# Up-projection groups in seven products: first sums of two groups in another tile, operand halves interleaved, one more group in the wide form

## The chip, the cores and the metric

The kernel runs on one core of one Trainium2 chip. Its engines run side by side, each in the order of its own instruction list: TensorE (PE, with its weight loads shown as PEld), VectorE (DVE), ScalarE (ACT), GpSimd (POOL) and SyncE (SP); the latter two mostly issue DMAs here. The metric is the device time of one execution in microseconds, the median over the runs.

## The reference

One layer of a streaming encoder on 512 tokens of width 1024, in float32: a mixing part (gated linear attention and forgetting attention side by side) and a feed-forward part. The change lies in the feed-forward part alone:

```python
a, val = jnp.split(rmsnorm(x, norm_ffn_g) @ w_up, 2, axis=-1)   # 1024 -> 2 x 2816
a = causal_dwconv(a, conv_w, conv_b)                            # width 3, along the tokens
return x + (jax.nn.gelu(a) * val) @ w_down                      # 2816 -> 1024
```

A final RMSNorm follows.

## The kernel before

**Precision.** Every float32 operand is split into a high and a low part (`hi` is a rounded copy, made on ScalarE; `lo` the difference, made on VectorE), and a product is three matmuls: high x high, high x low and low x high (`mm3`, lines 325 to 328). `split_next` (lines 270 to 303) does this for each piece of 1024 weight columns: a DMA brings the piece into a raw tile, line 291 casts it, line 292 subtracts. Three pairs of `wh` and `wl` tiles are in use at a time.

**The up-projection.** The 22 blocks of 128 features are worked as follows: two (`NCL`) in the plain way, `plain_products`; the other twenty in ten groups (`NSS`) of two blocks by a scheme with seven products in place of eight. x is cut in two halves of tokens (256 each, `H`) and two halves of features (four blocks of 128, `KH`), which gives x11, x12, x21, x22, and the weights are cut likewise. A step (g, p) is product p of group g: 24 matmuls of 256 columns in the narrow form (`up_product`, line 1443). Operands 1, 5, 3 lie in the tile `xo`, operands 2, 6, 7 in the tile `xw`, which held the halves `x2h` and `x2l` of x for the plain products, and operand 4 in `xc`; `split_x` (line 1337) fills them. The sums and differences y1 to y4 that some of them are made from lie in spare places of `act[0]`.

The program lists the steps by `SLOT`: (0,1), (0,5), (0,2), (0,3), (0,6), (1,1), (1,5), (0,7), (1,2), (0,4), (1,3), (1,6), (2,1) and so on. Small jobs are hung ahead of the first steps (`ahead_of`, line 1437): splits of operands, and the convolution, gelu and products of the two plain blocks. The order in which each engine gets its instructions is set when the program is built, by a planner that takes what it believes to be ready, earlier program lines first; it may put a later step ahead of an earlier one that waits.

**Accumulators.** Products 1 and 2 of a group add up in one accumulator ("x"), 5 and 3 in a second ("z"), 6, 7 and 4 in a third ("y"). "x" and "z" come from two pairs of PSUM banks (`pwide`), "y" from four single banks (`pmm`), which the plain blocks use at first. When a first product is done, `joint` (line 1468) copies the sums out, and the bank goes on to the second product. The first sums of x (p = 1) are needed in "y":

- In groups 0 and 1 they are copied into a part of `act[1]` (line 1534) and added to "y" when product 6 is done (line 1544).
- From group 2 on they are put into the bank of "y" ahead (line 1537).

`act[1]` is the tile that takes the activations of the second half of the blocks; it is first needed for them in group 4. It has the slot of the pool `x2pool` that the tile `xs` has before it, and `xs` holds x11 to x22; its last reader is the split of operand 4, hung ahead of (1,2). `s3` and `s4`, two more tiles of sums, have slots of their own; `s4` is first written for the blocks of `act[1]`.

**The wide form.** In groups 2 to 8 (`WIDE`) products 1, 2, 5 and 3 go through `wide_product` (line 1456). High and low half of the operand are streamed together as 512 columns against the high weights, and the high half once more as 256 columns against the low weights: 16 matmuls where the narrow form has 24. The result lies in two halves of a bank; `joint` copies one half out on ScalarE (line 1474) and adds the other on VectorE (line 1477). The two halves of an operand lie 1024 elements apart in `xo` and 3072 apart in `xw`.

**Afterwards.** The down-projection is done in seven products too. Its odd products take their operand from `ops[1]`, whose high part is the first 2816 elements of each partition of the first half of `xw` and whose low part those of its second half; `split_act` fills it (lines 1385 and 1386).

Of the kernel before, what the change touches and what calls it, by code (L numbers as in the profile page):

```python
# [9 lines left out]
F32R = mybir.dt.float32r  # L10
# [7 lines left out]
P = 128  # L18
T = 512
NT = T // P  # L20
D = 1024
KD = D // P
# [12 lines left out]
H = T // 2  # L35
KB = NF // 2
# [23 lines left out]
NCL = 2  # L60
NSS = (NF - NCL) // 2

WIDE = range(2, NSS - 1)
SLOT = {1: -1, 5: 0, 2: 2, 3: 4, 6: 5, 7: 8, 4: 10}

EARLY = (6, 7)
# [12 lines left out]
def c_of_piece(i):  # L79

    order = []
    for c in range(-GAHEAD, KD):
        order += ([None] if c + GAHEAD < KD else []) + ([c] if c >= 0 else [])
    return order[i] if i >= 0 else None
# [7 lines left out]
def hybrid_kernel(ctx: ExitStack, tc, xT, xt, wp, wu, wd, wf, wn, pp, aw2, fing, out):  # L92
    nc = tc.nc
    mm = nc.tensor.matmul
# [19 lines left out]
    def pmm():  # L114
        return bank("mm")

    def pax():
        return bank("ax")

    def pwide():  # L120
        return banks_of["wide"].tile([P, 2, 512], F32, tag="wide", name="ps_wide")
# [47 lines left out]
    for i, w in enumerate(wps[16:n_out]):  # L169
        fresh(w)  # L170
        c = c_of_piece(i - GH - KD)
# [147 lines left out]
    def piece(ahead=NW):  # L319
        n = taken[0]  # L320
        taken[0] += 1
        split_to(n + ahead + sum(i in spare for i in range(n, n + ahead)))
        return splits[n]
# [51 lines left out]
    for _ in range(NWARM):  # L375
        mm(  # L376
            warm, lhsT=nc.const_aps.tensor(1.0, (P, P), BF16), rhs=nc.const_aps.tensor(1.0, (P, T), BF16),
            start=True, stop=True,
# [59 lines left out]

    xpool = ctx.enter_context(tc.tile_pool(name="xpool", bufs=1))

    xw = xpool.tile([P, 2, (KD - 2) * T], F32R, name="xw")
    xab = [xw[:, i] for i in range(2)]
    xc = [xpool.tile([P, 1024], F32R, name=f"xc{i}") for i in range(2)]
    xh, xl = (
        [xab[i][:, k * T : (k + 1) * T] for k in range(KD - 2)] + [c[:, i * T : (i + 1) * T] for c in xc]
# [33 lines left out]
    first = [pmm(), pmm(), pmm(), pmm(), pax()]  # L479
# [335 lines left out]
    for tt in range(NT):  # L815
        for j in range(2):
            t = slice(tt * P, (tt + 1) * P)
            c = slice((2 * (tt % 2) + j) * P, (2 * (tt % 2) + j + 1) * P)
# [15 lines left out]
    for tt in range(NT):  # L834
        for j in range(2):
            for par in range(2):
                for c in range(2 * tt, min(2 * tt + 2, NC - 1)):
# [3 lines left out]
                        lhsT=kdt[r, tt, j, par * CH : (par + 1) * CH],  # L841
                        rhs=vg[r, tt, (2 * j + par) * GDV : (2 * j + par + 1) * GDV],
                        start=True, stop=True,
# [35 lines left out]
    for u in range(2):  # L879
        for par in range(2):  # L880
            for t2, j, c in quarters:
# [4 lines left out]
                    rhs=vg[:, 2 * u + t2, h * GDV : (h + 1) * GDV],  # L886
                    start=(t2 == j == 0), stop=False, skip_group_check=True,
                )
    for u in range(2):
        for t2, j, c in quarters:  # L890
            for par in range(2):
                r = slice(par * CH, (par + 1) * CH)
                for cp in range(2):
# [3 lines left out]
                        rhs=prev[r, j, ck, :], start=False, stop=True, skip_group_check=True,  # L897
# [171 lines left out]
    for i, run in enumerate(RUNS):  # L1069
        for unit in units[2 * i : 2 * i + 2]:  # L1070
            last = logits(*unit)
        for what in run:
# [4 lines left out]
            n = int(what[1:])  # L1077
# [43 lines left out]
    def minus_sum(out, a, b):  # L1121
        nc.vector.scalar_tensor_tensor(out=out, in0=a, scalar=-1.0, in1=b, op0=ALU.mult, op1=ALU.subtract)
# [17 lines left out]
    for c in range(-GAHEAD, KD):  # L1140
# [23 lines left out]
        else:  # L1164
            k = c - KD // 2
# [146 lines left out]
    for g in range(2):  # L1312
        n = at_step[g, 5]
# [13 lines left out]

    KH = KD // 2
    xo = npool.tile([P, 6 * KH * H], F32R, tag="xo", name="xo")
    places2 = [xo[:, i * 2048 : (i + 1) * 2048].rearrange("p (a n) -> p a n", a=2) for i in range(3)]  # L1330
    places2 += [xw[:, :, i * 1024 : (i + 1) * 1024] for i in range(3)]
    both = {p: x.rearrange("p a (k t) -> p a k t", t=H) for p, x in zip((1, 5, 3, 2, 6, 7), places2)}
    xops = {p: (x[:, 0], x[:, 1]) for p, x in both.items()}
    xops[4] = tuple(x.rearrange("p (k t) -> p k t", t=H) for x in xc)
    x11, x12, x21, x22 = (xs[:, j * KH : (j + 1) * KH, i * H : (i + 1) * H] for i in range(2) for j in range(2))

# [8 lines left out]
    def block(name, n=1, pool=npool):  # L1345
        return pool.tile([P, n, KB, H], F32, tag=name, name=name)

    act = [block("act1", 2)]
# [3 lines left out]
    s3, s4 = (block(f"s{i}")[:, 0] for i in (3, 4))  # L1352
# [35 lines left out]
    def convolve(f, i, t0):  # L1388
        nonlocal last_gelu
        nc.scalar.activation(  # L1390
            out=t0[:, i], in_=ap[:, i, 2 : T + 2], func=AF.Identity, scale=col(C_CW + 2 * NF + f), bias=col(C_CB + f)
        )
        for w in (1, 0):
            nc.vector.scalar_tensor_tensor(
                out=t0[:, i], in0=ap[:, i, w : w + T], scalar=col(C_CW + w * NF + f), in1=t0[:, i],
                op0=ALU.mult, op1=ALU.add,
            )
        with tc.issue_after(last_sigmoid.ins):
            last_gelu = nc.scalar.activation(out=t0[:, i], in_=t0[:, i], func=AF.Gelu_apprx_tanh)

    def halves(x):
        return x.rearrange("p (i t) -> p i t", t=H)

    def sums_of_acts(j, k):
        if j == 0:
            nc.vector.tensor_sub(out=s3[:, k], in0=a11[:, k], in1=a21[:, k])
            split_act(0, a11, k)
        else:
            nc.vector.tensor_sub(out=s1[:, k], in0=a22[:, k], in1=a21[:, k])
            minus_sum(s2[:, k], s1[:, k], a11[:, k])  # L1410
            minus_sum(s4[:, k], a12[:, k], s2[:, k])
# [44 lines left out]
    def wide_product(ps, p, first):  # L1456

        wh, wl = piece()
        for i in range(2):
            for k in range(KH):  # L1460
                c = slice((i * KH + k) * P, (i * KH + k + 1) * P)
                mm(ps[:, i], lhsT=wh[:, c], rhs=both[p][:, :, k], start=first and k == 0, stop=False, skip_group_check=True)  # L1462
                mm(  # L1463
                    ps[:, i, 0], lhsT=wl[:, c], rhs=both[p][:, 0, k], start=False, stop=k == KH - 1,
                    skip_group_check=True,
                )

    def joint(g, ps, out=None, tag="joint3"):

        if out is None or g in WIDE:  # L1470
            x = npool.tile([P, 2, H], F32, tag=tag, name=tag, bufs=2)
            out = out or [(x, slice(0, 2))]
        if g in WIDE:
            nc.scalar.copy(out=x, in_=ps[:, :, 1])
        for o, c in out:
            if g in WIDE:
                nc.vector.tensor_add(out=o, in0=ps[:, c, 0], in1=x[:, c])
            else:
                nc.scalar.copy(out=o, in_=halves(ps)[:, c])
        return out[0][0]  # L1480
# [29 lines left out]
    def parts_of(f):  # L1510
        if f // KB == (f + 1) // KB:
            return [(f // KB, slice(f % KB, f % KB + 2), slice(0, 2))]
        return [((f + i) // KB, slice((f + i) % KB, (f + i) % KB + 1), slice(i, i + 1)) for i in range(2)]

    st_of = {}
    for n, (g, p) in enumerate(steps):
        for what in ahead_of.get(n, ()):
            what()
        st = st_of.setdefault(g, {})
        f = NCL + 2 * g  # L1520
        name = {1: "x", 2: "x", 5: "z", 3: "z", 6: "y", 7: "y", 4: "y"}[p]
        first = name not in st
        if first:

            if name == "y":
                st[name] = pmm()
            elif g in WIDE:
                st[name] = pwide().rearrange("p i (a t) -> p i a t", t=H)
            else:
                st[name] = pwide()[:, 0]  # L1530
        ps = st[name]
        (wide_product if name != "y" and g in WIDE else up_product)(ps, p, first)
        if p == 1 and g < WIDE[0]:
            st[1] = joint(g, ps, [(act[1][:, 1, KB - 2 * g - 2 : KB - 2 * g], slice(0, 2))])
        elif p == 1:
            st["y"] = pmm()
            joint(g, ps, [(halves(st["y"]), slice(0, 2))])
        elif p == 2:
            joint(g, ps, [(act[j][:, 0, k], fs) for j, k, fs in parts_of(f)])
        elif p in (3, 5):  # L1540
            st[p] = joint(g, ps, tag=f"joint{p}")
        elif p == 6:
            if g < WIDE[0]:
                nc.vector.tensor_add(out=halves(ps), in0=halves(ps), in1=st[1])
            minus_sum(ap[:, :, 2 : H + 2], halves(ps), st[3])
        elif p == 7:
            minus_sum(ap[:, :, H + 2 : T + 2], halves(ps), st[5])
            t0 = st["t0"] = npool.tile([P, 2, T], F32, tag="t0", name="t0")
            for i in range(2):
                convolve(f + i, i, t0)  # L1550
        elif p == 4:
            t0 = st["t0"]
            for i in range(2):
                for j, k, fs in parts_of(f):
                    a = act[j][:, i, k]
                    nc.vector.tensor_mul(
                        out=a, in0=a if i == 0 else halves(ps)[:, fs], in1=t0[:, fs, i * H : (i + 1) * H]
                    )
            for j, k, _ in parts_of(f):
                sums_of_acts(j, k)  # L1560
        if g == NSS - 1 and p in EARLY:
            first_down(EARLY.index(p))
# [253 lines left out]
```

## Time and profile before

| | |
|---|---|
| median of 3 runs | 698.30 us (697.53 to 698.86) |
| the profiled execution, its own time | 697.54 us |
| its span, first to last instruction | 695.8 us |
| mean granted TensorE clock | 0.994 |
| VectorE busy from 375 to 399 us | 23.49 of 24.00 us |

In the answers of the trace times are microseconds from the span's start. A row of the timeline has the start and the length of an instruction, the engine, the line of the kernel, the operation, what it writes and reads, and in brackets the time that the engine sat idle before it and what ended that. Matmuls overlap, so the distance of their starts says what one costs. A row of the waits has the waiting instruction, what released it, the time in total, how often, and the longest.

### The profile page before, as it was taken

The numbers are of one execution on the slowest core, as the hardware profiler recorded it, in microseconds if no ns is written. First come the engines' busy times: TensorE is split into PE (matmuls) and PEld (weight loads), VectorE is DVE, ScalarE is ACT, GpSimd is POOL, SyncE is SP. The second block draws the span as 40 slices with busy tenths as digits, with TensorE's granted clock in tenths as the row PEclk, the third lists the DMA queues.
The fourth block names the chain that finished last, engine by engine and source line by source line (L and its number), as shares of the span: only waits on it lengthen the run. The fifth ranks groups of instructions, "written<-read, shape, count | busy, mean of one in ns | idle before, by whom it ended". The sixth has DMA issues, their size and how long they took to land.

```text
span 695.8 us, 10697 instructions
## 1 busy us (share of the span) xinstructions
PE 683.5 (98%) x3907; PEld 588.4 (85%) x3907; DVE 546.3 (79%) x852; ACT 432.1 (62%) x698; POOL 137.0 (20%) x196
## 2 busy tenths in 40 slices
PE   9999999999999999999999799999999999999996
PEld 6788888888888888888888799999999999888885
DVE  6774979867775766677679968888998879977884
ACT  7487676677768634335675566655666666555663
POOL 1125010123321324341010111211212102000122
PEclk9999999999999999999999899999999999999999
DMA  8769398988675499978973869999899988866643
GB/s 310 270 205 310 69 286 233 301 194 213 154 166 130 112 248 216 263 138 219 242 243 90 185 129 220 214 220 206 183 231 205 211 204 243 278 200 182 194 139 121
DMA packets 46184, 142.23 MB, mean 204 GB/s; under 512 B 5396, under 2 KB 9388, under 8 KB 46004
## 3 DMA queue, kind: packets, MB, share of 16 engines
q1 hardware_dynamic: 31156, 92.98, 39.6%
q0 software_dynamic: 11808, 43.52, 35.6%
q10 hardware_dynamic: 3168, 5.05, 2.1%
q8 instruction: 30, 0.49, 0.3%
q14 instruction: 22, 0.18, 0.1%
HBM read 137.32 MB, written 27.28 MB: 237 GB/s over the span
## 4 chain that ended last, share of the span: by engine, by line
PE 97%; ACT 1%; DVE 1%; issue 0%; DVEq 0%; ACTq 0%
PE ps_mm L326 20%; PE ps_mm L328 20%; PE ps_mm L327 20%; PE ps_wide L1462 8%; PE ps_wide L326 5%; PE ps_wide L327 5%; PE ps_wide L328 5%; PE ps_wide L1463 4%; PE ps_lg L1040 1%; PE ps_lg L981 1%; PE ps_pt L1015 1%; PE ps_mm L488 1%; PE ps_ax L326 1%; PE ps_ax L327 1%; PE ps_ax L328 1%; PE ps_ax L376 1%
## 5 line engine op out<-in xcount | busy, mean ns | idle before, releaser
L291 ACT CAST wh<-rawx 128x1024 fp32r<-128x1024 f32 x75 | 76.2, 1016 | 55.9 <-PE ps_mm L327 20.0
L326 PE MATMUL ps_mm<-xw,wh 128*128 128x512 f32 (+1 forms) x320 | 109.3, 341 | 0.0
L327 PE MATMUL ps_mm<-xw,wh 128*128 128x512 f32 (+1 forms) x320 | 107.8, 337 | 0.0
L328 PE MATMUL ps_mm<-xw,wl 128*128 128x512 f32 (+1 forms) x320 | 107.6, 337 | 0.0
L292 DVE TENSOR_TENSOR wl<-rawx,wh 128x1024 fp32r<-128x1024 f32 x75 | 88.2, 1177 | 16.4 <-ACT wh L291 16.2
L292 DVE TENSOR_TENSOR wl<-raw,wh 128x1024 fp32r<-128x1024 f32 x58 | 74.6, 1287 | 20.7 <-ACT wh L291 20.5
L291 ACT CAST wh<-raw 128x1024 fp32r<-128x1024 f32 x58 | 60.7, 1048 | 41.5 <-PE ps_mm L327 19.0
L326 PEld LDWEIGHTS ps_mm<-xw,wh 128*128 128x128 f32 x320 | 60.5, 189 | 8.2 <-issue 0.9
L328 PEld LDWEIGHTS ps_mm<-xw,wl 128*128 128x128 f32 x320 | 60.5, 189 | 6.4
L327 PEld LDWEIGHTS ps_mm<-xw,wh 128*128 128x128 f32 x320 | 60.6, 189 | 5.9 <-DVE xw L1250 0.2
L1462 PE MATMUL ps_wide<-xo,wh 128*128 128x512 f32 x168 | 60.0, 399 | 0.0
L292 DVE TENSOR_TENSOR wl<-rawz,wh 128x1024 fp32r<-128x1024 f32 x31 | 39.2, 1265 | 17.0 <-ACT wh L291 16.8
L299 POOL DMA_DIRECT2D rawx<-in_wu_dram x30 | 25.9, 865 | 120.6 <-DVE wl L292 84.8
L1463 PE MATMUL ps_wide<-xo,wl 128*128 128x256 f32 x168 | 47.2, 281 | 0.0
L326 PE MATMUL ps_mm<-xc,wh 128*128 128x256 f32 (+1 forms) x136 | 45.1, 331 | 0.0
L327 PE MATMUL ps_mm<-xc,wh 128*128 128x256 f32 (+1 forms) x136 | 44.6, 328 | 0.0
L328 PE MATMUL ps_mm<-xc,wl 128*128 128x256 f32 (+1 forms) x136 | 44.5, 327 | 0.0
L291 ACT CAST wh<-rawz 128x1024 fp32r<-128x1024 f32 x31 | 32.4, 1045 | 13.6 <-issue 5.0
L307 POOL COPY tick<-wl 128x1 f32<-128x1 f32 x37 | 10.9, 295 | 136.1 <-DVE wl L292 136.1
L1462 PEld LDWEIGHTS ps_wide<-xo,wh 128*128 128x128 f32 x168 | 31.6, 188 | 7.2
L326 PE MATMUL ps_mm<-wh,xw 128*128 128x512 f32 x96 | 37.7, 393 | 0.0
L327 PE MATMUL ps_mm<-wl,xw 128*128 128x512 f32 x96 | 37.4, 390 | 0.0
(490 smaller groups left out, 1859.1 us busy)
## 6 DMA issues: line engine op xcount, KB each, us to landing
rawx<-in_wu_dram POOLq DMA_DIRECT2D x40, 512.0 KB, 6.7
rawz<-in_wp_dram SPq DMA_DIRECT2D x30, 512.0 KB, 5.3
raw<-in_wp_dram SPq DMA_DIRECT2D x22, 512.0 KB, 5.0
wsum<-in_wd_dram SPq DMA_DIRECT2D x20, 512.0 KB, 6.7
rawx<-in_wu_dram SPq DMA_DIRECT2D x20, 512.0 KB, 5.1
raw<-in_wu_dram SPq DMA_DIRECT2D x20, 512.0 KB, 4.5
rawx<-wsum SPq DMA_DIRECT2D x12, 512.0 KB, 4.5
wsum<-in_wd_dram POOLq DMA_DIRECT2D x10, 512.0 KB, 8.0
```

Of the source, the lines that this page charges most:

```text
L291: nc.scalar.copy(out=hi[:, :m], in_=raw[:, :m])
L292: nc.vector.tensor_sub(out=lo[:, :m], in0=raw[:, :m], in1=hi[:, :m].bitcast(F32))
L299: nc.gpsimd.dma_start(raw, recipes[i][0], accum_op=ALU.add)
L307: now = nc.gpsimd.tensor_copy(out=tick, in_=lo[:, 0:1].bitcast(F32))
L326: mm(ps, lhsT=ah, rhs=bh, start=start, stop=False, **k)
L327: mm(ps, lhsT=ah, rhs=bl, start=False, stop=False, **k)
L328: mm(ps, lhsT=al, rhs=bh, start=False, stop=stop, **k)
L376: mm(warm, lhsT=nc.const_aps.tensor(1.0, (P, P), BF16), rhs=nc.const_aps.tensor(1.0, (P, T), BF16), start=True, stop=True,)
L488: mm(first[i], lhsT=w[:, i * P : (i + 1) * P], rhs=x, start=(k == j == 0), stop=False)
L981: last = mm(lg[:, place_of_q(qb)], lhsT=a[r, q], rhs=b[r, :n], start=(j == 0), stop=(j == 2))
L1462: mm(ps[:, i], lhsT=wh[:, c], rhs=both[p][:, :, k], start=first and k == 0, stop=False, skip_group_check=True)
L1463: mm(ps[:, i, 0], lhsT=wl[:, c], rhs=both[p][:, 0, k], start=False, stop=k == KH - 1, skip_group_check=True,)
```

## The change

Three edits.

1. The first sums of groups 0 and 1 go into `s4` (elements 0 to 1 of its second axis for group 0, 2 to 3 for group 1) in place of `act[1]`. The bound of this way of handling them is now `PRELOADED = 2`, apart from `WIDE`.
2. `xw` becomes one flat tile, and each operand that the wide form can take lies as block, half, token: for each block of 128 features 256 elements of the high half and then 256 of the low half. `split_x` writes, and the narrow form reads, every other run of 256; the wide form's 512 columns are one run. Operand 2 now takes the first third of `xw`, 6 the second, 7 the last; before, each took a third of both halves.
3. `WIDE` begins with group 1. Group 1's products 1, 2, 5 and 3 are wide, and their joints have a copy and an add.

```diff
-WIDE = range(2, NSS - 1)
+WIDE = range(1, NSS - 1)
+PRELOADED = 2
...
-    xw = xpool.tile([P, 2, (KD - 2) * T], F32R, name="xw")
-    xab = [xw[:, i] for i in range(2)]
+    xw = xpool.tile([P, 2 * (KD - 2) * T], F32R, name="xw")
+    xab = [xw[:, i * (KD - 2) * T : (i + 1) * (KD - 2) * T] for i in range(2)]
...
-    places2 = [xo[:, i * 2048 : (i + 1) * 2048].rearrange("p (a n) -> p a n", a=2) for i in range(3)]
-    places2 += [xw[:, :, i * 1024 : (i + 1) * 1024] for i in range(3)]
-    both = {p: x.rearrange("p a (k t) -> p a k t", t=H) for p, x in zip((1, 5, 3, 2, 6, 7), places2)}
-    xops = {p: (x[:, 0], x[:, 1]) for p, x in both.items()}
+    places2 = [t[:, i * 2048 : (i + 1) * 2048] for t in (xo, xw) for i in range(3)]
+    both = {p: x.rearrange("p (k a t) -> p k a t", a=2, t=H) for p, x in zip((1, 5, 3, 2, 6, 7), places2)}
+    xops = {p: (x[:, :, 0], x[:, :, 1]) for p, x in both.items()}
...
-                mm(ps[:, i], lhsT=wh[:, c], rhs=both[p][:, :, k], start=first and k == 0, stop=False, skip_group_check=True)
+                mm(ps[:, i], lhsT=wh[:, c], rhs=both[p][:, k], start=first and k == 0, stop=False, skip_group_check=True)
                 mm(
-                    ps[:, i, 0], lhsT=wl[:, c], rhs=both[p][:, 0, k], start=False, stop=k == KH - 1,
+                    ps[:, i, 0], lhsT=wl[:, c], rhs=both[p][:, k, 0], start=False, stop=k == KH - 1,
...
-        if p == 1 and g < WIDE[0]:
-            st[1] = joint(g, ps, [(act[1][:, 1, KB - 2 * g - 2 : KB - 2 * g], slice(0, 2))])
+        if p == 1 and g < PRELOADED:
+            st[1] = joint(g, ps, [(s4[:, 2 * g : 2 * g + 2], slice(0, 2))])
...
-            if g < WIDE[0]:
+            if g < PRELOADED:
                 nc.vector.tensor_add(out=halves(ps), in0=halves(ps), in1=st[1])
```

## The prediction, made before the changed kernel ran

> **What bounds the kernel now.** I read the page first: the span, the busy shares, the chain that ended last.
>
> ```profile
> span 695.8 us, 10697 instructions
> PE 683.5 (98%) x3907; PEld 588.4 (85%) x3907; DVE 546.3 (79%) x852; ACT 432.1 (62%) x698; POOL 137.0 (20%) x196
> PE 97%; ACT 1%; DVE 1%; issue 0%; DVEq 0%; ACTq 0%
> ```
>
> TensorE is busy 98% and the chain runs through it for 97%, so an edit is worth what it takes out of TensorE's stream, or out of the few holes in it. The second view is therefore TensorE's list of waits. Its two longest entries are these, and both lie in the stretch that the change touches:
>
> ```profile
> PE ps_wide L326 <- ACT act L1479: 4.2, 1, 4.2
> PE ps_wide L326 <- ACT joint L1479: 1.4, 1, 1.4
> ```
>
> The third view is the timeline of TensorE from the first up-projection step to the first one of group 2. Columns: start, length, engine, line, what.
>
> ```profile
> 376.23 0.28 PE L326 MATMUL ps_wide<-xo,wh 128*128 128x256 f32 x1
> 376.34 0.28 PE L327 MATMUL ps_wide<-xo,wh 128*128 128x256 f32 x1
> 376.46 0.28 PE L328 MATMUL ps_wide<-xo,wl 128*128 128x256 f32 x1
> ...
> 383.54 0.39 PE L326 MATMUL ps_wide<-xo,wh 128*128 128x256 f32 x1 [1.40 <-ACT joint L1479]
> ...
> 396.60 0.58 PE L326 MATMUL ps_wide<-xw,wh 128*128 128x256 f32 x1 [4.17 <-ACT act L1479]
> ...
> 400.61 0.41 PE L326 MATMUL ps_wide<-xw,wh 128*128 128x256 f32 x1
> 400.82 0.41 PE L327 MATMUL ps_wide<-xw,wh 128*128 128x256 f32 x1
> 401.04 0.33 PE L328 MATMUL ps_wide<-xw,wl 128*128 128x256 f32 x1
> ...
> 419.04 0.40 PE L1462 MATMUL ps_wide<-xo,wh 128*128 128x512 f32 x1
> ```
>
> Three things are to be seen. Matmuls of 256 columns start 0.12 us apart, so a narrow product of 24 takes 2.88 us. The order is not that of the list of steps: after (0,1), (0,5) come (0,3), (0,6), (1,1), and (0,2), the first to read `xw`, comes only at 396.60. And after the hole of 4.17 us the matmuls start 0.21 us apart, up to 401.04: 20 intervals in 4.44 us where 2.40 would do, a loss of 2.04 us. After the hole of 1.40 us nothing is slowed.
>
> From 376.23 to 419.04 TensorE does the twelve products of groups 0 and 1: 42.81 us, of which 12 x 2.88 = 34.56 is work. **The stretch loses 8.25 us**: 1.40 + 4.17 idle, 2.04 at the slow clock, and 0.64 of drain and restart at the holes. Why the long hole is there, the timelines of ScalarE and VectorE say:
>
> ```profile
> 394.72 1.21 DVE L1341 TENSOR_TENSOR xc<-xs,xc 128x1024 fp32r<-128x1024 f32 x1
> 395.97 1.07 ACT L1479 COPY act<-ps_wide 128x512 f32<-128x512 f32 x2 [2.52 <-DVE xc L1341]
> ```
>
> The first of the two copies at 395.97 is the joint of (0,1), whose product was over by 379.1. It writes into `act[1]`, which shares its slot with `xs`, and so it waits for the last reader of `xs`, the split of operand 4 on VectorE. (0,2) accumulates in the bank that this copy reads, so it waits too; (0,7) waits behind line 1544, which needs the same sums, and (1,5) for the bank of (0,2). That wait, not VectorE's or TensorE's rate, ends last here.
>
> **The change part by part.** *First sums to `s4`.* `s4` has a slot of its own, and nothing in the kernel writes or reads it before group 4. The joint of (0,1) can then run on ScalarE as soon as the product ends, at 379.1 plus one 1.05 us cast in front of it; (0,2) needs the split of operand 2, and follows (0,5) at 382.0. What is late next? VectorE, busy nearly all the time from here:
>
> ```profile
> 376.23:382.00 5.77, 5.77 (x49) 5.70 (x47) 5.77 (x6) 5.77 (x8) 0.87 (x1) 1.00 0.55 123
> 382.00:392.30 10.30, 8.90 (x74) 8.70 (x72) 9.85 (x12) 8.51 (x11) 1.79 (x3) 1.00 0.97 213
> 392.30:401.56 9.26, 5.09 (x26) 4.96 (x25) 6.72 (x9) 2.63 (x4) 0.79 (x1) 0.63 0.53 126
> 401.56:419.04 17.48, 17.48 (x147) 17.33 (x145) 12.64 (x15) 11.33 (x15) 2.77 (x4) 1.00 0.72 146
> 419.04:439.11 20.07, 20.07 (x139) 18.58 (x138) 17.24 (x22) 12.54 (x17) 3.64 (x5) 1.00 0.91 209
> ```
>
> The columns are the stretch, its length, and the busy time of PE, PEld, DVE, ACT and POOL, then granted clock, DMA share and GB/s. VectorE does 34.98 us of work in the first four rows. The change adds four adds (line 1477) for the four wide products of group 1. The next rows give its prices:
>
> ```profile
> 380.08 1.21 DVE L1341 TENSOR_TENSOR xw<-xs,xw 128x1024 fp32r<-128x1024 f32 x1
> 381.21 1.21 DVE L292 TENSOR_TENSOR wl<-rawx,wh 128x1024 fp32r<-128x1024 f32 x1
> ...
> 391.85 0.69 DVE L1427 TENSOR_TENSOR ps_mm<-ps_mm,rb 128x512 f32<-128x512 f32 x1
> ...
> 396.58 0.70 DVE L1544 TENSOR_TENSOR ps_mm<-ps_mm,act 128x512 f32<-128x512 f32 x1
> 397.19 0.68 DVE L1406 TENSOR_TENSOR s<-act 128x512 f32<-128x512 f32 x1
> ...
> 410.28 2.73 DVE L1394 SCALAR_TENSOR_TENSOR t<-ap,ppt,t 128x512 f32<-128x512 f32 x4
> ...
> L1477 DVE TENSOR_TENSOR joint<-ps_wide,joint x14: 680/682/684, 427.0 to 558.7; 128x512 f32<-128x512 f32 x14
> ```
>
> By starts, a 1024-wide instruction holds VectorE for 1.13 us, a 512-wide one for 0.6, the four of a convolution for 2.65. I walk its queue on from 391.85, up to where I leave it as it was: line 1544 of group 0 and 1122 (1.25), operand 7 and the weights of (0,7) (2.26): 395.4, and TensorE, unbroken since 376.23, comes to (0,7) at 396.4. Then add (1,1), weights (1,2), add (1,5), 1427, weights (0,4), 1122, operand 4 (4 x 0.6 + 3 x 1.13 = 5.79): 401.2, needed at 402.1. Convolution and weights of (1,3) (3.78): 404.9, needed at 405.0. Add (1,2), 1430, weights (1,6) (2.33): 407.3, needed at 407.9. Two of 1556, 1406, 1386, weights of (2,1) (3.53): 410.8, needed at 410.7. So TensorE is met everywhere to within 0.1 us: the stall shrinks from 8.25 to a few tenths. As bounds: VectorE has 34.98 + 4 x 0.6 = 37.4 us to do in 34.5 us; if nothing can be put off TensorE waits 2.9 us, if the 2.4 us of 1556, 1406, 1386 and the 1.13 of (2,5)'s weights are put off, 33.9 is left and it waits for nothing. I take **0.5 us**, near the walk. In the last row VectorE needs 17.24 of the 20.07 us of a group, so a backlog of 2.9 is gone after one group.
>
> ScalarE (28.24 us) fits with room. The DMAs of these twelve steps keep their triggers and their order on SP and POOL (a split frees a raw tile, SP loads and POOL adds into it), and come earlier with the splits.
>
> ```profile
> rawx<-in_wu_dram POOLq DMA_DIRECT2D x40, 512.0 KB, 6.7
> ```
>
> The nearest case is (1,6): its weights are added into the tile of (1,5), split at 391.85, land 6.7 us after the issue, near 399, and are cast for 407.8. The DMA share over the four rows is 0.72 on average, 0.89 if the stretch is 34.5 us long, below the 0.91 of the last row, in which TensorE was never idle. I price them at nothing.
>
> *Group 1 wide.* From the last row a group with four wide and three narrow products takes 20.07 us, so a wide one takes (20.07 - 3 x 2.88) / 4 = 2.857 us, 0.023 less than a narrow one. The columns streamed are the same (512 + 256 against 3 x 256). Four of them: **-0.09 us**. The price is the adds, counted above, which stand in front of the release of their bank.
>
> *Halves interleaved.* The wide matmul's moving operand becomes one run of 512 instead of two of 256. What would that buy?
>
> ```profile
> L1462 PE MATMUL ps_wide<-xo,wh x168: 395/398/403, 419.0 to 555.3; 128*128 128x512 f32 x168
> ...
> 584.23 0.28 PE L328 MATMUL ps_mm<-xw,wl 128*128 128x256 f32 x1
> 584.35 0.40 PE L326 MATMUL ps_wide<-wh,acth 128*128 128x512 f32 x1
> ...
> 585.97 0.39 PE L327 MATMUL ps_wide<-wl,acth 128*128 128x512 f32 x1
> ...
> 222.14 0.39 PE L1040 MATMUL ps_lg<-ph,v 128*128 128x512 f32 x1
> 222.37 0.39 PE L1040 MATMUL ps_lg<-pl,v 128*128 128x512 f32 x1
> ```
>
> The two-run matmul of line 1462 takes 0.398, some 0.009 more than the 0.39 of other 512-wide ones. But the one-run matmul at 584.35, behind a 256-wide one as each of line 1462 is, takes 0.40 too, and line 1040's at 222.14, whose operand also has two runs, takes 0.39. So the excess goes with what stands before, not with the runs. I take 0; the bound is 256 x 0.009 = -2.3 us. The splits write in runs of 256 now; line 1341 above reads `xs` in such runs at full rate, so 0; TensorE's cover for a change there is VectorE's margin in the walk.
>
> *Operands under the last splits.* The low half of the down operand now lies where operands 6 and 7 are, not 2, 6 and 7. Two early splits on VectorE must move:
>
> ```profile
> 368.60 1.22 DVE L1370 TENSOR_TENSOR act<-xs 128x1024 f32<-128x1024 f32 x1
> ...
> 572.16 0.95 DVE L1386 TENSOR_TENSOR xw<-act,xw 128x768 fp32r<-128x768 f32 x1
> ...
> 581.36 0.95 DVE L1386 TENSOR_TENSOR xw<-act,xw 128x768 fp32r<-128x768 f32 x1
> ...
> 578.73 0.40 PE L326 MATMUL ps_wide<-wh,acth 128*128 128x512 f32 x1
> ...
> 599.52 0.39 PE L326 MATMUL ps_mm<-wh,xw 128*128 128x512 f32 x1
> ```
>
> They wait for (9,6) and (9,7) to end, at 578.73 and 584.35, where first down products start; first wanted at 599.52. Cost 0, hidden by those 15 us; bound 0.9, one of them in front of weights that TensorE then misses.
>
> **Sum**: -8.25 + 0.5 - 0.09 = -7.84 us. The profiled execution took 697.54 us, so 689.7; the median of the runs, 698.3, stands 0.76 above it, so **690.5 us**.
>
> **The rivals.** *A, the forecast*, 690.5, from 690.0 (no stall left) to 691.5; chance 0.58. *B, VectorE becomes the bound*: its queue orders what can be put off ahead of weights. For it speaks that the walk's margins are 0.1 us at (1,3) and below zero at (2,1); against it that the backlog lasts one group. 2.9 us of stall instead of 0.5: 692.9; up to 694.9 if it comes in one hole that also slows the clock by 2 us as above. Chance 0.22. The Trainium skill (page "TensorE: Matmul & The Clock Gate", section "Part 1: The HAM clock gate") says that the clock is halved after an idle window of about 3.4 us and comes back after as much work. The holes here agree with it (1.40 no, 4.17 yes, then 0.21 us for 4.4 us); by that rule B's hole of 2.9 would stay at the full clock and 692.9 would hold. *C, the single run is faster*: 0.009 us each, 2.3 us more: 688.2. For it the 0.398, against it line 1040 and 584.35. Chance 0.12. The Trainium skill (page "PSUM — Partial Sum Buffer", section "Specifications (TRN2)") says that any non-contiguous access pattern slows matmuls significantly; it speaks of PSUM, where line 1462 writes one run already, and only taken for the operand as well would it mean C. *D, the change doesn't do what it says*: the step list's order on TensorE stays, because (0,2) is held by another of its inputs until about 396: 698.2, chance 0.04. *E, slower*: the first copy into `s4` comes no earlier than 396.0, held by a former tenant of that place as `act[1]` is by `xs`. Then the stall stays whole, and the joints of group 1 release their banks one add (0.68) later, on top of the 0.9 of the last splits: +1.6 - 0.09, 699.8. Against it: `act[0]`, a tile of the same pool, is written at 368.60 without a wait. Chance 0.04.
>
> **How the numbers follow.** 688.0 to 693.5 holds A, B at its likely price and C: 0.8 and somewhat more. Faster by over 0.2% (1.4 us, about what a measurement of this kernel can tell from no change): A, B, C, 0.92; within it, D, 0.04; slower, E, 0.04.
>
> **What would show it.** Right: the joint of (0,1) starts near 380 and writes `s`; (0,2) follows (0,5) on TensorE with no hole; the entry of 4.2 is gone from the waits and the granted clock is 1.00 from 376 on; line 1462 has 256 matmuls, first near 390; the first matmul of (2,1) starts near 411. Wrong: a new wait of TensorE on VectorE's line 292 or 1477 (B); line 1462 at 0.389 (C); the first write of `s` after 390 (E); a hole between 578 and 605, which would mean the moved splits.

## The result, and the profile after

| | before | after |
|---|---|---|
| median (range, runs), us | 698.44 (697.53 to 698.86, 4) | 689.94 (689.68 to 691.07, 4) |
| ratio after/before, 95% interval | | 0.9883 (0.9866 to 0.9900) |
| profiled execution, its span, us | 697.54, 695.8 | 689.94, 688.2 |
| mean granted TensorE clock | 0.994 | 0.998 |

The kernel became 8.5 us faster (1.2%); the forecast was 690.5. The line numbers of the up-projection code are one higher than before up to line 1329, so that line 326 is now 327. The page, its span, its busy shares and its chain:

```profile
span 688.2 us, 10637 instructions
...
PE 681.4 (99%) x3875; PEld 585.0 (85%) x3875; DVE 547.8 (80%) x856; ACT 431.5 (63%) x698; POOL 135.5 (20%) x196
...
PE 99%; DVE 1%; issue 0%; ACT 0%; DVEq 0%; ACTq 0%
```

TensorE now fills the chain to 99%, and ScalarE has left it. The list of TensorE's waits, columns as before (total, times, longest), has a single row left, and it lies long before the changed part:

```profile
PE ps_ax L377 <- PEq L1803: 0.9, 1, 0.9
```

The timelines of the changed stretch say what became of the hole. First ScalarE, then TensorE at the start of each new step:

```profile
379.66 0.58 ACT L1479 COPY s<-ps_wide 128x512 f32<-128x512 f32 x1
```

```profile
376.52 0.28 PE L327 MATMUL ps_wide<-xo,wh 128*128 128x256 f32 x1
...
382.27 0.28 PE L327 MATMUL ps_wide<-xw,wh 128*128 128x256 f32 x1
...
390.91 0.39 PE L1462 MATMUL ps_wide<-xo,wh 128*128 128x512 f32 x1
391.39 0.39 PE L1463 MATMUL ps_wide<-xo,wl 128*128 128x256 f32 x1
391.62 0.39 PE L1462 MATMUL ps_wide<-xo,wh 128*128 128x512 f32 x1
...
396.92 0.28 PE L327 MATMUL ps_mm<-xw,wh 128*128 128x256 f32 x1
...
411.20 0.40 PE L1462 MATMUL ps_wide<-xo,wh 128*128 128x512 f32 x1
```

The copy of (0,1)'s sums runs at 379.66, where before it ran at 395.97, and writes `s`, which is `s4` (the profile leaves out the numbers of names). (0,2) starts at 382.27 behind (0,5), 14.3 us earlier than before. With that the hole of 1.40 us went too: (0,3), which stood there waiting for the copy of (0,5)'s sums, now comes behind (0,2), at 385.15, and that copy runs at 382.75. The wide steps begin at 390.91 with (1,1), (0,7) comes at 396.92, and group 2 at 411.20. From the first step to there it is 34.68 us in place of 42.81: 8.13 us less.

The whole difference can be laid out by three points of the trace: the first step, the first step of group 2, and the first down product (578.73 before, 571.14 after).

| us | before | after | difference |
|---|---|---|---|
| up to the first step | 376.23 | 376.52 | +0.29 |
| groups 0 and 1, to (2,1) | 42.81 | 34.68 | -8.13 |
| to the first down product | 159.69 | 159.94 | +0.25 |
| to the end of the span | 117.07 | 117.06 | -0.01 |
| span | 695.80 | 688.20 | -7.60 |

The windows of after, with the columns as in the prediction, show what comes next to the bound:

```profile
376.52:411.20 34.68, 34.59 (x257) 32.83 (x256) 33.54 (x39) 27.72 (x36) 6.23 (x8) 1.00 0.86 187
```

```profile
411.20:419.96 8.76, 8.76 (x58) 7.84 (x57) 8.76 (x13) 4.12 (x5) 1.05 (x2) 1.00 0.77 188
```

The clock is 1.00 throughout. VectorE is busy 33.54 of 34.68 us in the stretch and 8.76 of 8.76 in the three products behind it: the hole of TensorE is gone, and VectorE works at the edge of being late.

### The profile page after: what moved, and what is told of

Its sections match the earlier page's. It is cut to its first block, busy times and chain, and to the rows that moved or that the text cites. A ratio compares the mean times of both kernels' runs of the same rounds, so it can differ in the third digit from the quotient of the medians.

```text
span 688.2 us, 10637 instructions
## 1 busy us (share of the span) xinstructions
PE 681.4 (99%) x3875; PEld 585.0 (85%) x3875; DVE 547.8 (80%) x856; ACT 431.5 (63%) x698; POOL 135.5 (20%) x196
## 4 chain that ended last, share of the span: by engine, by line
PE 99%; DVE 1%; issue 0%; ACT 0%; DVEq 0%; ACTq 0%
PE ps_mm L327 20%; PE ps_mm L329 20%; PE ps_mm L328 20%; PE ps_wide L1462 9%; PE ps_wide L327 5%; PE ps_wide L329 5%; PE ps_wide L328 5%; PE ps_wide L1463 4%; PE ps_lg L1041 1%; PE ps_lg L982 1%; PE ps_pt L1016 1%; PE ps_mm L489 1%; PE ps_ax L327 1%; PE ps_ax L328 1%; PE ps_ax L329 1%; PE ps_ax L377 1%
## 5 line engine op out<-in xcount | busy, mean ns | idle before, releaser
L1462 PE MATMUL ps_wide<-xo,wh 128*128 128x512 f32 x192 | 68.6, 399 | 0.0
L1463 PE MATMUL ps_wide<-xo,wl 128*128 128x256 f32 x192 | 54.1, 282 | 0.1
L1462 PEld LDWEIGHTS ps_wide<-xo,wh 128*128 128x128 f32 x192 | 36.1, 188 | 8.2
L327 PE MATMUL ps_mm<-wh,xw 128*128 128x512 f32 x96 | 37.7, 393 | 0.0
L329 PE MATMUL ps_mm<-wh,xw 128*128 128x512 f32 x96 | 37.4, 389 | 0.0
```

What stands on the lines that cost most here:

```text
L327: mm(ps, lhsT=ah, rhs=bh, start=start, stop=False, **k)
L329: mm(ps, lhsT=al, rhs=bh, start=False, stop=stop, **k)
L1462: mm(ps[:, i], lhsT=wh[:, c], rhs=both[p][:, k], start=first and k == 0, stop=False, skip_group_check=True)
L1463: mm(ps[:, i, 0], lhsT=wl[:, c], rhs=both[p][:, k, 0], start=False, stop=k == KH - 1, skip_group_check=True,)
```

## The experiments

Two questions had to be told apart: which of the three edits makes the gain, and whether the cause is the slot of `act[1]`, or something else that came with the edits. The theory: the slot alone makes it, and VectorE is the next bound. The rivals: the interleaved operand or the wide group 1 carries part of the gain; or (0,2) was held by another input.

**One part alone: the slots.** The kernel before, with the first sums in `s4`:

```diff
+PRELOADED = 2
...
-        if p == 1 and g < WIDE[0]:
-            st[1] = joint(g, ps, [(act[1][:, 1, KB - 2 * g - 2 : KB - 2 * g], slice(0, 2))])
+        if p == 1 and g < PRELOADED:
+            st[1] = joint(g, ps, [(s4[:, 2 * g : 2 * g + 2], slice(0, 2))])
...
-            if g < WIDE[0]:
+            if g < PRELOADED:
```

> The kernel before with the first sums of groups 0 and 1 in s4, and nothing else of the change. Theory S (the slot is the whole gain): the copy of (0,1)'s sums starts near 380, the 4.2 us and 1.4 us entries are gone from TensorE's waits, the stretch from the first step to the first matmul of (2,1) falls from 42.81 to about 34.7 us (12 x 2.88 = 34.56 plus at most 0.5), the time to 690.2 to 691.0. Rival W (the fewer matmuls of the wide group and the single run of its operand bring the gain, the slot is only their condition): 696 to 698.5.

690.1 us (689.64 to 690.66), ratio 0.9877 (0.9863 to 0.9892). The copy of (0,1)'s sums comes at once (this kernel's line 1480 is line 1479 above), and the window of the stretch, first step to (2,1), is as short:

```profile
380.23 0.58 ACT L1480 COPY s<-ps_wide 128x512 f32<-128x512 f32 x1
```

```profile
377.09:411.91 34.82, 34.80 (x289) 34.59 (x288) 33.84 (x39) 27.91 (x36) 6.29 (x9) 1.00 0.84 184
```

34.82 us, 0.14 more than with all three edits, and a median that the interval does not tell from theirs. The slots alone make the whole gain.

**One part alone: the interleave.** The kernel before, with `xw`, `places2`, `both`, `xops` and the wide matmuls' operands as in the change, and `WIDE` and the slots as before:

```diff
-    both = {p: x.rearrange("p a (k t) -> p a k t", t=H) for p, x in zip((1, 5, 3, 2, 6, 7), places2)}
+    both = {p: x.rearrange("p (k a t) -> p k a t", a=2, t=H) for p, x in zip((1, 5, 3, 2, 6, 7), places2)}
...
-                mm(ps[:, i], lhsT=wh[:, c], rhs=both[p][:, :, k], start=first and k == 0, stop=False, skip_group_check=True)
+                mm(ps[:, i], lhsT=wh[:, c], rhs=both[p][:, k], start=first and k == 0, stop=False, skip_group_check=True)
```

> The kernel before with the halves interleaved, and nothing else of the change. Theory S: both holes stay (4.2 and 1.4 us), a wide group takes 20.07 us as before, the 512-wide matmuls 0.398, the time 697.5 to 699.3. Rival W (a single run streams faster): 0.389 each, 224 x 0.009 = 2.0 us less, 696.4. Third possibility, that the splits into every other run of 256 or the later low halves of the last splits cost something: 1.04 or 1.13 becomes longer by starts, or a hole opens between 578 and 605, 699 to 700.

698.11 us, ratio 0.9995 (0.9985 to 1.0004): no change. The holes stay, as the waits of TensorE say, and the group of 512-wide matmuls (count, busy, mean ns, idle before) has its old duration:

```profile
PE ps_wide L327 <- ACT act L1479: 4.6, 1, 4.6
PE ps_wide L327 <- ACT joint L1479: 1.4, 1, 1.4
```

```profile
L1462 PE MATMUL ps_wide<-xo,wh 128*128 128x512 f32 x168 | 60.0, 399 | 0.0
```

Here one run of 512 is no faster than two of 256 as a moving operand.

**The slots undone.** The changed kernel, with `act[1]` again; interleave and wide group 1 stay:

```diff
-            st[1] = joint(g, ps, [(s4[:, 2 * g : 2 * g + 2], slice(0, 2))])
+            st[1] = joint(g, ps, [(act[1][:, 1, KB - 2 * g - 2 : KB - 2 * g], slice(0, 2))])
```

> The changed kernel with the first sums back in act[1] (group 1 wide, halves interleaved). Theory S: the hole before (0,2) is back with 4 us and the half clock behind it; four adds of 0.6 us on VectorE lie where it idled (3.7 and 3.5 us before 402.7 and 407.4), so 697.9 to 699.0. The slower case of the prediction gave 699.8 for this (banks released one add later, and the moved splits). Rival W: at least half the gain stays, below 695.

697.86 us, ratio 0.9989 (0.9980 to 0.9999). The gain is gone. On the timeline, ScalarE's copy and TensorE's (0,2) stand where they stood before the change:

```profile
396.49 0.58 ACT L1479 COPY act<-ps_wide 128x512 f32<-128x512 f32 x1 [2.17 <-DVE xc L1341]
```

```profile
397.13 0.58 PE L327 MATMUL ps_wide<-xw,wh 128*128 128x256 f32 x1 [4.30 <-ACT act L1479]
```

Without the slots the other two edits are together worth 0.7 us against the kernel before on this chip (698.56), by the interval 0.1 to 1.4. In the profiled executions it is 0.81 us less from the first step to the first down product, and 0.72 of that is (0,2), which spent less time at the slow clock (4.24 us in place of 4.96).

**Group 1 narrow again.** The changed kernel with one bound as before:

```diff
-WIDE = range(1, NSS - 1)
+WIDE = range(2, NSS - 1)
```

> The changed kernel with group 1 narrow again (slots in s4, halves interleaved). Theory S: within 0.5 us of the changed kernel, 689.5 to 690.7; the stretch up to (2,1) is 34.56 to 34.8 us, VectorE has four adds (2.4 us) less to do in it. Rival W: 4 us or more slower than the changed kernel, 694 or above.

689.87 us, ratio 0.9874 (0.9859 to 0.9888): as with group 1 wide. The windows of the stretch and of the three products behind it:

```profile
376.21:411.12 34.91, 34.80 (x290) 34.60 (x288) 33.81 (x39) 27.91 (x36) 6.25 (x9) 1.00 0.85 190
```

```profile
411.12:419.65 8.53, 8.53 (x58) 7.78 (x57) 6.77 (x9) 4.12 (x5) 1.02 (x2) 1.00 0.93 248
```

Group 1 narrow costs 0.23 us in the stretch (34.91 against 34.68, and 0.1 over the 34.8 expected at most) and gets 0.23 back behind it (8.53 against 8.76): 43.44 us in both. In the second window VectorE has the two adds of group 2 either way. With group 1 wide it also has work there that the adds of group 1 pushed back, such as lines 1406 and 1386, twice each: 8.76 us in all, where narrow it has 6.77.

**Is it the last reader of `xs`?** Two runs leave the sums in `act[1]` and move that reader instead, the split of operand 4. In the first it is hung ahead of step 3 of the list, in the second ahead of step 5; both start from the kernel before, with it at step 8.

```diff
-        1: (lambda: split_x(2, x12, third),), 3: (lambda: split_x(6, y2, third), plain_gelus),
-        4: (lambda: plain_values(0),), 5: (lambda: plain_act(0), p7_operand), 8: (lambda: split_x(4, x22, third),),
+        1: (lambda: split_x(2, x12, third),), 3: (lambda: split_x(6, y2, third), lambda: split_x(4, x22, third), plain_gelus),
+        4: (lambda: plain_values(0),), 5: (lambda: plain_act(0), p7_operand),
```

> The kernel before, first sums still in act[1], but the split of operand 4 hung ahead of (0,3) in place of (1,2). Theory S (what holds the copy of (0,1) is the last reader of xs): the last reader is now line 1433, over about 391, so the copy starts at 391 to 392 and (0,2) at 392 to 393, right behind (1,1); the hole of 4.2 us falls under 1 us and the slow clock is gone, the hole of 1.4 us stays, the stretch up to (2,1) is 36.2 to 37.5 us, the time 691.5 to 693.5. Rival P (not the slot but the planner's order, (0,2) behind (1,1), makes the loss): nothing gained, 697.5 to 699.5.

692.5 us, ratio 0.9923 (0.9906 to 0.9939); the stretch took 37.14 us. The copy now waits for what has become the last reader, `p7_operand` (line 1433 reads `xs`, at 390.15):

```profile
391.40 0.59 ACT L1479 COPY act<-ps_wide 128x512 f32<-128x512 f32 x1 [0.31 <-DVE act L1433]
```

```diff
-        4: (lambda: plain_values(0),), 5: (lambda: plain_act(0), p7_operand), 8: (lambda: split_x(4, x22, third),),
+        4: (lambda: plain_values(0),), 5: (lambda: plain_act(0), p7_operand, lambda: split_x(4, x22, third)),
```

> The kernel before with the split of operand 4 hung right behind the operand of product 7, ahead of (1,1): the order on TensorE is that of the kernel before, VectorE does this split two instructions (2.27 us) earlier, so the hole before (0,2) should be 4.17 - 2.27 = 1.9 us. Theory C (the half clock needs a hole longer than some 3 us): the matmuls behind it start 0.12 us apart, the stretch falls by 2.27 + 2.04 = 4.3 to about 38.5 us, the time to 694.1 plus or minus 0.5. Rival (any hole of that kind slows the clock): only 2.3 us gained, 696.2.

693.48 us, ratio 0.9942 (0.9923 to 0.9960); the stretch took 38.23 us. The hole, expected at 1.9 us, was 1.55. The split on VectorE, the copy behind a cast on ScalarE, and TensorE's (0,2):

```profile
392.59 1.22 DVE L1341 TENSOR_TENSOR xc<-xs,xc 128x1024 fp32r<-128x1024 f32 x1
...
393.15 1.04 ACT L291 CAST wh<-rawx 128x1024 fp32r<-128x1024 f32 x1 [0.52 <-PE ps_wide L327]
394.10 1.07 ACT L1479 COPY act<-ps_wide 128x512 f32<-128x512 f32 x2
...
394.73 0.39 PE L326 MATMUL ps_wide<-xw,wh 128*128 128x256 f32 x1 [1.55 <-ACT act L1479]
```

So the copy moves with the last reader of `xs`: it comes at 391.40, 394.10 and, before, 395.97. In the first of the two runs and before, it starts within 0.04 us of that reader's end (391.37 and 395.93, the start and length of its row). In the second the reader ends at 393.81, and the last 0.29 us are the cast in front of the copy. Behind this hole of 1.55 us (0,2) took 2.98 us, the full rate but for 0.1; behind the 4.17 us of before, matmuls stood 0.21 us apart for 4.44 us.

**More work for VectorE.** The changed kernel with group 0 wide too, which adds four more adds:

```diff
-WIDE = range(1, NSS - 1)
+WIDE = range(0, NSS - 1)
```

> The changed kernel with group 0 wide as well. TensorE's work falls by another 4 x 0.023 = 0.09 us; VectorE gets four more adds (2.4 us) into a stretch in which it was busy 33.56 of 34.70 us. Theory V (VectorE was just about at the bound): 1 to 2.5 us of waits for VectorE appear on TensorE, each shorter than 3 us and without a slow clock, 690.8 to 692.3. Rival (enough can be put off): the stretch stays within 0.3 us of 34.68, 689.5 to 690.5.

692.14 us, ratio 0.9917 (0.9902 to 0.9931): 2.2 us slower than the changed kernel, though TensorE has no more to do. The two ran at different times, but the traces say the same: from the first step to the first down product 196.96 us against 194.62. The waits of TensorE:

```profile
PE ps_mm L328 <- DVE xw L1341: 0.6, 1, 0.6
PE ps_mm L327 <- ACT xw L1339: 0.6, 1, 0.6
PE ps_mm L329 <- DVE wl L293: 0.4, 1, 0.4
PE ps_wide L1462 <- DVE s L1477: 0.3, 1, 0.3
```

Three of the four rows are operands or weights that come late from VectorE or the cast ahead of it, the last an add of line 1477. The stretch took 36.60 us. Rival B of the prediction is real, one group further on.

**Is the excess of a 512-wide matmul that of its predecessor?** The changed kernel with a wide product's eight 512-wide matmuls first and then its eight 256-wide ones:

```diff
                 mm(ps[:, i], lhsT=wh[:, c], rhs=both[p][:, k], start=first and k == 0, stop=False, skip_group_check=True)
+        for i in range(2):
+            for k in range(KH):
+                c = slice((i * KH + k) * P, (i * KH + k + 1) * P)
                 mm(
```

> The changed kernel with the eight 512-wide matmuls of a wide product first and the eight 256-wide ones behind them, instead of in turn. Theory K (a 512-wide matmul loses some 9 ns when it stands behind a 256-wide one, whatever the runs of its operand): a wide product takes 8 x 0.2268 + 8 x 0.12 + 0.03 = 2.80 us in place of 2.857, a group 19.85 in place of 20.07, 32 products 1.5 to 1.8 us: 688.2 to 688.6. Rival (the 9 ns go with the operand or with the bank): 20.07 stays, 689.5 to 690.3.

690.12 us, ratio 0.9886 (0.9870 to 0.9903): missed, no gain. The matmul group, a group's window and the one new wait:

```profile
L1462 PE MATMUL ps_wide<-xo,wh 128*128 128x512 f32 x192 | 48.1, 392 | 0.0
```

```profile
440.46:460.27 19.81, 19.81 (x138) 18.47 (x137) 16.98 (x21) 12.39 (x16) 3.67 (x5) 1.00 0.96 239
```

```profile
417.90 0.39 PE L329 MATMUL ps_mm<-xw,wl 128*128 128x256 f32 x1 [1.17 <-DVE wl L293]
```

The 512-wide ones fall from 399 to 392 ns, as the prediction's reading of the excess had it. But a group gains only 0.12 us, not the 0.22 expected, because the 20.07 us it was reckoned from was wrong (below); and TensorE, a little earlier, waits 1.17 us in (1,7), right behind the stretch, for weights from VectorE, which takes it back: from the first step to the first down product it is 194.81 us against 194.62.

**The same with group 1 narrow**, where VectorE has time in that place, beside the changed kernel again on the same chip:

```diff
-WIDE = range(1, NSS - 1)
+WIDE = range(2, NSS - 1)
```

> Slots in s4, halves interleaved, group 1 narrow, and the wide products of groups 2 to 8 with their 512-wide matmuls first. Theory K and V together (the reordering takes 19.93 to 19.81 us per group; with group 1 wide VectorE's backlog gave it back in a wait of 1.2 us in group 2): without group 1's adds no wait of TensorE after 376 us, seven groups x 0.12 = 0.85 us less than with group 1 narrow in turn (689.87), so 689.0, and some 0.9 below the changed kernel on the same chip. Rival (the gain per group is lost elsewhere in any case): equal to the changed kernel within 0.3 us, with a new wait on VectorE's line 293.

> The changed kernel once more, to stand beside the run above on one chip: 689.9 within 0.7 us; a group of the steady part 19.93 us, the stretch up to (2,1) 34.7 us.

689.41 us (688.92 to 689.69), ratio 0.9871 (0.9855 to 0.9887), beside 691.21 (689.97 to 691.59), ratio 0.9892 (0.9878 to 0.9907), for the changed kernel. That one lies above the 689.2 to 690.6 expected of it, and the difference of 1.8 us is twice the 0.9 expected. The new wait is gone. The two profiled executions took 688.92 and 691.59 us, their spans 687.2 and 689.9, 2.70 us apart: 0.43 up to the first step, 0.79 from there to the first down product (193.74 against 194.53), and 1.48 behind it. In that last part the changed kernel had a wait in this execution, near its end:

```profile
671.28 0.50 PE L328 MATMUL ps_wide<-wl,acth 128*128 128x512 f32 x1 [1.03 <-DVE wl L293]
```

It was not in the changed kernel's first profile, and why it comes in some executions stays open. Of the difference only the middle part belongs to the edit for sure. So the order was weighed once more, with group 1 narrow in both:

> The changed kernel with group 1 narrow, again, as the measure for the run that follows on the same chip. If the order of a wide product's matmuls is worth what the trace of the run before showed (0.86 us up to the first down product), this one has 194.6 us from the first step to the first down product and a median 0.7 to 1.0 us above the next. If that difference was one of chip and moment, the two medians agree to 0.3 us.

> The same with the 512-wide matmuls of each wide product first. 193.7 us from the first step to the first down product, and a median 0.7 to 1.0 us below that of the run before it, if the order is worth 0.12 us per group of four wide products in seven groups; within 0.3 us of it if not.

690.28 us (690.00 to 690.53) for the old order, 689.29 (688.97 to 689.97) for the new one, four runs of each and no overlap: 0.99 us. To the first down product 194.51 and 193.68 us, so 0.83 of it lies in the seven wide groups, as 7 x 0.12. So the order by width is worth 0.14% where VectorE has room.

## Why the prediction was right, point by point

**The bound and the cause were read rightly.** TensorE's stream sets the time, and the hole came from the slot that `act[1]` takes over from `xs`. The slots alone give the gain, undoing them alone takes it, and the copy came earlier in both runs that moved the last reader of `xs`, in one of them right at its end.

**The sum.** Forecast -7.84 us against the profiled execution, measured -7.60. That the two are so near is partly luck: the stretch gained 8.13, 0.29 more than forecast, and as much was lost before the first step, where nothing was changed, and 0.25 behind the stretch. The 0.76 us put on top for the median did not show: the profiled execution after, 689.94, is itself at the median. Term by term:

- *The stall, -8.25, and 0.5 left over.* Forecast for the stretch: 34.56 + 0.5 - 0.09 = 34.97 us; measured 34.68. What is left is 0.36 us, all in one place: the first matmul of line 1463 in (1,1) starts 0.48 us behind that of line 1462, where elsewhere in the product it is 0.24, and the next follows 0.23 later, where it is 0.11. It waits for its low weights, whose split ended at 391.34:

```profile
390.12 1.22 DVE L293 TENSOR_TENSOR wl<-raw,wh 128x1024 fp32r<-128x1024 f32 x1
```

  The engine was the right one, the place was not: the walk of VectorE's queue began only at 391.85 and took the order before it from the kernel before. With group 1 narrow the same weights cost as much: 0.39 us and then 0.22 between matmuls that stand 0.12 apart elsewhere. So this rest does not come from the adds.
- *VectorE's deadlines.* The walk had the weights of (0,7) at 395.4 and the step at 396.4; they ended at 396.2 and the step came at 396.92. For the end it had weights of (2,1) at 410.8 for a start at 410.7; they came at 409.4, because the planner put them ahead of the adds of line 1556, not behind:

```profile
408.27 1.22 DVE L293 TENSOR_TENSOR wl<-raw,wh 128x1024 fp32r<-128x1024 f32 x1
409.41 0.69 DVE L1556 TENSOR_TENSOR act<-act,t 128x512 f32<-128x512 f32 x1
```

  That is what rival B needed the other way round.
- *Group 1 wide, -0.09.* This term was mis-sized. The prediction took the window from 419.04 to 439.11 for one group. Its start is that of (2,1), but (3,1) starts before its end, as the timeline of the kernel before shows:

```profile
438.97 0.40 PE L1462 MATMUL ps_wide<-xo,wh 128*128 128x512 f32 x1
```

  So a group takes 438.97 - 419.04 = 19.93 us, and one (2,2) to (3,2) the same. A wide product is then (19.93 - 3 x 2.88) / 4 = 2.823 us, and the term -0.23. That much appears in the stretch. It was given back behind it, where VectorE had no room: in (1,7), the third product of the window from 411.20, TensorE's first matmul with low weights came 0.13 us late and the next one another 0.10. With group 1 narrow, TensorE runs through there without a pause. The edit's net is zero, not -0.09.
- *Interleave, 0, with a bound of -2.3.* Zero it was: 398 ns for line 1462, and no change when it was made alone. What stands before, guessed at 9 ns from three rows, is 7 ns in the mean length of a matmul (399 to 392). By starts it is less: 0.12 us a group over 32 such matmuls, some 4 ns each.
- *The last splits, 0, with a bound of 0.9.* They moved to 572.01, 576.60 and 585.93, and TensorE has no hole from 570 to 600:

```profile
570.00:600.00 30.00, 30.00 (x161) 25.99 (x161) 29.22 (x38) 18.95 (x25) 3.01 (x4) 1.00 0.83 275
```

**The rivals.** B came only as tenths of a microsecond, 0.36 in (1,1) and 0.23 in (1,7), not as its 2.9; one group more of adds brings it. Its argument that a hole of 2.9 us would stay at the full clock is not borne out: in the trace of the kernel before, the granted clock was down to 0.50 already 1.9 us into the hole (last section). No run had a hole of that length. C falls with the 398 ns. D falls with 382.27. E falls with 379.66; the run with the old slots did not show its price either (697.86, not 699.8).

## What to carry to other kernels

In this kernel a tile that takes over a slot waits for the last reader of the tile before it, even if the part written now was never in use (`xs` fills the first 4096 of the slot's 5632 elements; group 0's sums went to those from 5120 on): look for early, small results in a tile that is meant for later, and give them one with a slot of its own. When the hole of a bounding engine goes, walk the queue of the next engine against deadlines from the first step on, not only from the hole. Take the length of a repeated group from one step to the same step one group on; a window that ends elsewhere carries its offset into every number worked out from it.

## What the runs showed of the hardware

Holes of 1.40 us (before) and 1.55 us (split of operand 4 moved) left TensorE at the full rate. Those of 4.17 us (before), 4.30 (old slots put back) and 4.59 (interleave alone) did not: the granted clock stood at 0.50 behind them, matmuls of 256 columns started 0.21 us apart, and (0,2) took 4.96, 4.24 and 4.98 us rather than 2.88. No run had a hole between 1.55 and 4.17 us.

The Trainium skill (page "TensorE: Matmul & The Clock Gate", section "Part 1: The HAM clock gate") puts the point at an idle window of about 3.4 us. As the length of a hole these traces do not bear that out. Read in windows of 0.2 us, the granted clock fell to 0.50 some 1.9, 3.8 and 2.3 us after the three holes began, and came back some 6.8, 3.4 and 6.8 us after it fell. So the loss behind a hole did not go by its length: 2.08 us behind that of 4.17, 1.36 behind that of 4.30, 2.10 behind that of 4.59. What sets the moment of the fall stays open.

A 512-wide matmul behind a 256-wide one is listed with 399 ns on average; with eight of them in a row the average is 392. By starts, ordering a product of eight and eight by width is worth 0.03 us, or 0.12 us for a group of four.
